# First block's up projection by seven block products, its context work moved, and token tiles taken in pairs

## The chip, the cores and the metric

The kernel runs on one core of a Trainium2 chip, in one launch. The metric is device time in microseconds, the lower the better; three runs of the kernel before took 2593.44, 2595.51 and 2596.91 us, so its median is 2595.51 us.

## The reference, cut to what matters

Two transformer blocks run one after the other over 1024 tokens of width 1024, all in fp32. What the change touches:

```
# first block
mix = token_mixer(x)                          # attention, then y @ w_out
x1  = layer_norm(ALPHA * x + mix)
u   = x1 @ w_up                               # 1024 x 5632: 22 chunks of value, 22 of gate, 128 wide
u   = u[t]*w2 + u[t-1]*w1 + u[t-2]*w0 + b     # causal convolution of width 3 along the tokens
x2  = layer_norm(ALPHA * x1 + (value * gelu(gate)) @ w_down)
# second block
shift, scale, gate ... = modulation of a conditioning vector (6 x 1024 sums)
h   = rmsnorm(x2) * g * (1 + scale) + shift   # then gated linear attention, two directions, whose
                                              # start states come from 256 context tokens
x   = x2 + gate * (gla(h) @ w_o)
x   = x + gate2 * (relu(norm(x) @ w1)**2 @ w2) ; out = rmsnorm(x) * final_g
```

## The kernel before, in words

Every matrix product is done with operands cut in two rounded halves (`split`: one copy on ScalarE gives the high half, one subtraction on VectorE the low half), and `mm3` (lines 131 to 133) issues three matmuls for one product: high by high, high by low and low by high. One 128-row step of a product over 512 columns is so three matmuls.

The program is one stream of stages. (1) Attention, to about 503 us. (2) `mixed`: the product with w_out by token tile (`square_product`, 2 halves of the columns, 8 tiles of 128 tokens, 24 matmuls each), and beside it `context`, the start states from the context tokens; behind each tile's second half comes its layer norm and the transposed halves `hi` and `lo` (lines 828 to 837). (3) `ffn`: for each of 22 chunks the two up products (`up`, line 855: 8 row steps by 2 halves by 3 matmuls, 48 for one 128-wide column chunk), the convolution from PSUM (lines 911 to 913), gelu and product, and in groups of three chunks the down product (`down`, line 864), which adds into the 8 resident tiles `res`. The modulation sums (`ada`) go out in small bits behind each chunk's convolution. The last group runs by tile and feeds the norm and the first values of stage (4), the gated linear attention. (5) `o_projection`: the product with w_o and the operands of the next stage, tiles 0 to 7 in order. (6) `mlp_up`: the second block's up projection, two 128-wide chunks at a time as a 2 by 2 block matrix times the 2 by 2 blocks of the activations, by seven block products of 12 matmuls (84 for a pair of chunks) where plain products would take eight (96). It needs sums and differences of the blocks, made on VectorE (`operands` and lines 1237 to 1242); the partial results go through the two output tiles `ga` and `gb`, which alternate between two sets of `res` tiles. (7) `mlp_down`, groups of four chunks read back from DRAM.

The order of instructions on each engine is laid down by the framework's planner, which takes the program order as priority and simulated times for what is ready. Each engine runs its queue in order; PE waits where a PSUM bank is still to be read. Tile pools are stacked, and a pool that is opened takes over the space of the one closed; with `reuse_waits="tile"` a tile waits only for the tiles that lay in its own bytes. The steps that the change touches: `mixed` 817 to 842, `up` and `down` 855 to 893, `ffn` 895 to 1005, `o_projection` 1127 to 1187, `mlp_up` 1211 to 1266, `mlp_down` 1271 to 1318.

Of the kernel before, what the change touches and what calls it, by code (L numbers as in the profile page):

```python
# [17 lines left out]
P = 128  # L18
D = 1024
# [35 lines left out]
def build(tc, I, out, dbg=None, stop=None):  # L55
# [41 lines left out]
    hi = actp.tile([P, KD, T], F32R, name="act_hi")  # L97
    lo = actp.tile([P, KD, T], F32R, name="act_lo")
# [459 lines left out]
    rawp, wp = pool(w_st, "wraw2", 4), pool(w_st, "wsplit2", 4)  # L558
# [62 lines left out]
    def square_product(wname, wo, done, scale=None, ks=range(KD)):  # L621

        W = I[wname]
        for half in range(2):
            ws = []
            for k in ks:
                r = wo.tile([P, 512], F32, tag="raw", name="woraw", bufs=2)
                SP.dma_start(out=r, in_=W[k, half])
                h = wo.tile([P, 512], F32R, tag="h", name="woh")
                l = wo.tile([P, 512], F32R, tag="l", name="wol")  # L630
                split(r, h, l, None if scale is None else scale[:, k:k + 1])
                ws.append((h, l))
            for t in range(NT):
# [4 lines left out]
                yield 5200  # L638
# [104 lines left out]
    def context(st):  # L743

        nonlocal gc, gt, ge, gv, gs
        gc = pool(st, "cc", 1)
        gt, ge, gv, gs = (pool(st, n, b) for n, b in (("gtc", 2), ("gec", 4), ("gvc", 4), ("gsc", 2)))
# [4 lines left out]
        for t in range(2):  # L752
            x, f = res[6], res[7]
# [63 lines left out]
    def mixed():  # L817
        st = ExitStack()
        set_banks(st, "m", {"c": (1, 2, "z hps fp tokp"), "ct": (1, 1, "ctp ktp dS"), "tp": (1, 2, "xtp"), "sq": (1, 3, "sq")})
        wo = pool(st, "wo", 8)  # L820
        aux = pool(st, "aux", 1)
# [6 lines left out]
        def done(t, half, psum):  # L828
            c = slice(half * 512, half * 512 + 512)
            if half == 0:  # L830
                mv[t] = aux.tile([P, 6], F32, name=f"mv{t}")
                SP.dma_start(out=res[t], in_=I["x"][toks(t), :])
                POOL.tensor_scalar(out=res[t], in0=res[t], scalar1=ALPHA, scalar2=0.0, op0=ALU.mult, op1=ALU.add)
            add_sum(res[t][:, c], psum, res[t][:, c], mv[t][:, half:half + 1])
            if half == 1:
                layer_norm(res[t], mv[t], g, b, junk, POOL if t < 6 else DVE)
                transposed(res[t], t)

        merge([(square_product("w_out", wo, done, ks=(4, 5, 6, 7, 0, 1, 2, 3)), 83200), (context(st), CTXSHARE)])
        st.close()  # L840

    mixed()

    def dump_res(key):
        for t in range(NT):
            SP.dma_start(out=dbg[key][toks(t), :], in_=res[t])
        ctx.close()

    if stop == "x1":
        return dump_res("x1")  # L850
# [4 lines left out]
    def up(w, name):  # L855
        w = w_get(w)
        psum = acc("up", T)
        for half in range(2):
            c = slice(half * 512, half * 512 + 512)
            for k in range(KD):  # L860
                mm3(psum[:, c], *w[k], hi[:, k, c], lo[:, k, c], k == 0, k == KD - 1)
        return psum

    def down(chs, g, wds, wdr, wdp, evac, tile_outer, by_col=None):
        def load(ch, half):
            r = wdr.tile([P, 512], F32, tag="r", name="wdraw")
            SP.dma_start(out=r, in_=wds[2 * ch + half])
            if by_col is not None:
                POOL.tensor_tensor(out=r, in0=r, in1=by_col[:, half * 512:half * 512 + 512], op=ALU.mult)
            h = wdp.tile([P, 512], F32R, tag="h", name="wdh")  # L870
            l = wdp.tile([P, 512], F32R, tag="l", name="wdl")
            split(r, h, l)
            return h, l

        def one(t, half, ws):
            psum = acc("down")
            for n, ch in enumerate(chs):
                gh, gl = g[ch]
                mm3(psum, gh[:, toks(t)], gl[:, toks(t)], *ws[n], n == 0, n == len(chs) - 1)
            evac(t, half, psum)  # L880

        if tile_outer:
            ws = [[load(ch, half) for ch in chs] for half in range(2)]
            for t in range(NT):
                for half in range(2):
                    one(t, half, ws[half])
                yield t
        else:
            for half in range(2):
                ws = [load(ch, half) for ch in chs]  # L890
                for t in range(NT):
                    one(t, half, ws)
                yield half

    def ffn():
        st = ExitStack()
        set_banks(st, "f", {"mm": (1, 2, "down"), "tp": (1, 2, "xtp ada"), "big2": (2, 1, "up tokp"), "big": (2, 1, "up tokp")})
        wdp = pool(st, "wdp", 6)
        ar = pool(st, "ar", 2)
        ac = pool(st, "ac", 1)  # L900
        gp = pool(st, "gp", 4)
        wdr = pool(st, "wdr", 2)
        cp = pool(st, "cp", 2)
        Wu, Wd = wlist("w_up"), wlist("w_down")
        groups = [list(range(i, min(i + 3, NCH))) for i in range(1, NCH, 3)]
        groups = [[0]] + groups

# [506 lines left out]
```

## Time and profile before

| what | us |
|---|---|
| median of 3 runs | 2595.51 |
| the profiled execution | 2593.83 |
| its span, first to last instruction | 2592.1 |
| PE busy in it | 2513.0 |
| VectorE (DVE) busy | 1471.6 |
| ScalarE (ACT) busy | 1053.2 |
| GpSimd (POOL) busy | 437.8 |

A row of the windows view gives a stretch of the span, its length, and for each engine the busy time and the number of instructions; PEclk is the clock that TensorE was granted as a share of full speed. A row of the view by line gives source line, engine, operation, output and inputs by the program's names, shape and count, then the busy time in us and the mean of one in ns, then the idle time of that engine just before these instructions and what ended it. In a timeline the first two numbers are start and duration in us. A matmul's duration overlaps with the next; its cost in a full stream is the distance of starts.

### The profile page before, as it was taken

Reading aid. Unit: us, or ns where it says so; the run is one execution under the profiler, and the core shown is the slowest. Engines: PE = TensorE matmul, PEld = TensorE weight load, DVE = VectorE, ACT = ScalarE, POOL = GpSimd, SP = SyncE. Lnnn points to the kernel's source line nnn. Section 1 sums busy time; section 2 is a strip of 40 time slices with the busy share of each in tenths; the row PEclk is TensorE's granted clock in tenths of the full one; section 3 lists DMA queues with packets and bytes.
Section 4 is the critical chain, followed back from the end, with each engine's and each line's share of the span. In section 5 each row is a group of like instructions: output and inputs, shape, how many; then the busy total and the mean of one; then the engine's idle time right before and its main releaser. Section 6 shows DMA issues by size and latency. Waiting matters only on the chain.

```text
span 2592.1 us, 35515 instructions
## 1 busy us (share of the span) xinstructions
PE 2513.0 (97%) x13114; PEld 2134.0 (82%) x13114; DVE 1471.6 (57%) x2757; ACT 1053.2 (41%) x1956; POOL 437.8 (17%) x583
## 2 busy tenths in 40 slices
PE   8999999899999999999998999999969999899998
PEld 7898988788788888888887888998858888688887
DVE  5767666758564555455557856444374444344466
ACT  5555555745221222222226644333355454421212
POOL 4675622423000000000006100000110000000023
PEclk9999999999999999999999999999989999999999
DMA  5334231532322222222222110112323232532222
GB/s 173 98 96 112 78 82 49 168 114 78 102 88 70 75 79 68 67 83 69 76 73 86 54 37 32 32 44 62 117 90 122 98 106 90 203 103 93 99 100 102
DMA packets 124718, 231.13 MB, mean 89 GB/s; under 512 B 15608, under 2 KB 47992, under 8 KB 124544
## 3 DMA queue, kind: packets, MB, share of 16 engines
q1 hardware_dynamic: 124544, 228.86, 27.5%
q8 instruction: 103, 1.69, 0.3%
q14 instruction: 71, 0.58, 0.1%
HBM read 185.25 MB, written 35.16 MB: 85 GB/s over the span
## 4 chain that ended last, share of the span: by engine, by line
PE 60%; issue 31%; DVE 3%; POOL 2%; DMA 2%; ACT 1%; SPq 0%; POOLq 0%; DVEq 0%; ACTq 0%
PE down L131 5%; PE down L132 5%; PE down L133 5%; PE s L131 4%; PE s L133 4%; PE s L132 4%; PE proj L131 3%; PE proj L133 3%; PE proj L132 3%; PE tokp L132 2%; PE tokp L133 2%; PE tokp L131 2%; PE y L416 2%; PE ptp L91 2%; PE sq L131 1%
## 5 line engine op out<-in xcount | busy, mean ns | idle before, releaser
L131 PE MATMUL down<-wdh,gh 128*128 128x512 f32 x864 | 338.8, 392 | 12.0 <-ACT gh L103 11.0
L132 PE MATMUL down<-wdl,gh 128*128 128x512 f32 x864 | 338.0, 391 | 0.3 <-DVE wdl L104 0.2
L133 PE MATMUL down<-wdh,gl 128*128 128x512 f32 x864 | 334.1, 390 | 0.2 <-DVE gl L104 0.2
L103 ACT CAST wh<-raw 128x512 fp32r<-128x512 f32 (+2 forms) x204 | 125.9, 622 | 416.1 <-PE up L132 366.7
L131 PE MATMUL up<-act_hi,wh 128*128 128x512 f32 x704 | 279.1, 397 | 3.3 <-DVE conv L913 2.5
L132 PE MATMUL up<-act_lo,wh 128*128 128x512 f32 x704 | 278.4, 395 | 0.0
L133 PE MATMUL up<-act_hi,wl 128*128 128x512 f32 x704 | 277.5, 394 | 0.0
L570 POOL TENSOR_TENSOR rstd<-rstd,mhalf 128x1 f32<-128x1 f32 x74 | 50.2, 678 | 1247.1 <-DVE rstd L569 1230.4
L104 DVE TENSOR_TENSOR wl<-raw,wh 128x512 fp32r<-128x512 f32 (+2 forms) x204 | 155.3, 769 | 158.9 <-ACT wh L103 152.3
L131 PEld LDWEIGHTS down<-wdh,gh 128*128 128x128 f32 x864 | 162.8, 188 | 48.6 <-ACT gh L103 11.5
L132 PEld LDWEIGHTS down<-wdl,gh 128*128 128x128 f32 x864 | 162.9, 189 | 35.2 <-DVE wdl L104 1.3
L133 PEld LDWEIGHTS down<-wdh,gl 128*128 128x128 f32 x864 | 162.2, 188 | 34.7 <-DVE gl L104 0.6
L131 PEld LDWEIGHTS up<-act_hi,wh 128*128 128x128 f32 x704 | 133.2, 189 | 33.0 <-ACT conv L911 2.9
L133 PEld LDWEIGHTS up<-act_hi,wl 128*128 128x128 f32 x704 | 133.1, 189 | 30.1
L132 PEld LDWEIGHTS up<-act_lo,wh 128*128 128x128 f32 x704 | 133.1, 189 | 29.6 <-DVE act_lo L615 0.4
L131 PE MATMUL tokp<-wh,act_hi 128*128 128x256 f32 (+1 forms) x512 | 148.0, 290 | 0.0
L132 PE MATMUL tokp<-wl,act_hi 128*128 128x256 f32 (+1 forms) x512 | 147.6, 289 | 0.0
L133 PE MATMUL tokp<-wh,act_lo 128*128 128x256 f32 (+1 forms) x512 | 146.5, 287 | 0.0
L1289 DVE TENSOR_TENSOR res<-res,down 128x512 f32<-128x512 f32 x112 | 76.7, 685 | 115.7 <-PE down L133 115.5
L103 ACT CAST wdh<-wdraw 128x512 fp32r<-128x512 f32 x108 | 65.6, 621 | 166.6 <-PE down L133 75.0
L922 DVE TENSOR_TENSOR res<-res,down 128x512 f32<-128x512 f32 x96 | 65.4, 686 | 111.8 <-PE down L133 111.6
L370 ACT ACTIVATE P<-P,mx 128x640 f32<-128x640 f32 (+7 forms) x128 | 94.4, 738 | 78.9 <-DVE mx L367 74.1
(325 smaller groups left out, 6209.4 us busy)
## 6 DMA issues: line engine op xcount, KB each, us to landing
ada_w<-in_ada_w SPq DMA_DIRECT2D x192, 128.0 KB, 2.1
raw<-in_w_up SPq DMA_DIRECT2D x88, 256.0 KB, 2.6
res<-in_mlp_w SPq DMA_DIRECT2D x32, 512.0 KB, 3.6
gd<-res SPq DMA_DIRECT2D x32, 512.0 KB, 4.2
wdraw<-in_mlp_w SPq DMA_DIRECT2D x64, 256.0 KB, 3.7
gload<-gd SPq DMA_DIRECT2D x32, 512.0 KB, 4.3
wdraw<-in_w_down SPq DMA_DIRECT2D x44, 256.0 KB, 2.7
raw<-in_wqk SPq DMA_DIRECT2D x32, 256.0 KB, 3.0
```

What stands on the lines that cost most here:

```text
L91: PE.transpose(out=o, in_=a, identity=ident)
L103: ACT.copy(h, raw)
L104: DVE.tensor_tensor(out=l, in0=raw, in1=h, op=ALU.subtract)
L131: PE.matmul(out=o, lhsT=ah, rhs=bh, start=first, stop=False, **kw)
L132: PE.matmul(out=o, lhsT=ah, rhs=bl, start=False, stop=False, **kw)
L133: PE.matmul(out=o, lhsT=al, rhs=bh, start=False, stop=last, **kw)
L370: ACT.activation(Pm[:, 0:W], Pm[:, 0:W], AF.Exp, bias=mx[:, 0:1], scale=-1.0, accum_out=mx[:, 1:2])
L416: PE.matmul(out=o, lhsT=lhsT, rhs=part[:, off:off + w], start=(first and n == 0 and m == 0), stop=(last and n == len(cur) - 1 and m == 1))
L570: POOL.tensor_tensor(out=t[:, 1:2], in0=t[:, 0:1], in1=mhalf, op=ALU.pow)
L922: DVE.tensor_tensor(out=r, in0=r, in1=psum, op=ALU.add)
L1289: DVE.tensor_tensor(out=r, in0=r, in1=psum, op=ALU.add)
```

## The change

The first block's up projection becomes the same seven-product routine as the second block's (`up_pass`, shared by both), as a pass of its own over 22 pairs (value chunk, gate chunk). Its results are written to DRAM (`g1d`), and the down product becomes a pass behind it (`down_group`, shared too) that reads them back, with groups of 2, 2 and six of 3 chunks. The context states and the modulation leave the w_out stage and the up pass and run beside the first seven groups of that down pass; the activations `hi` and `lo` are given up after the up pass and allocated anew. The layer norm's output goes to DRAM (`x1d`) and is added in the last group but one. In the two stages that make the operands, token tiles run as 0, 4, 1, 5, 2, 6, 3, 7, so that each pair's operands can be made as soon as both tiles are there; part of their work goes from VectorE and ScalarE to GpSimd. The first weight chunk of each up pass is loaded and split ahead into a pool of its own (`w0`). In the second block the gate vector multiplies the columns of w_o instead of the result. The pools of both down passes stand in another order.

```diff
+    PAIRED = (0, 4, 1, 5, 2, 6, 3, 7)
+    def square_product(wname, wo, done, scale=None, by_col=None, ks=range(KD)):
...
+                if by_col is not None:
+                    POOL.tensor_tensor(out=r, in0=r, in1=by_col[:, half * 512:half * 512 + 512], op=ALU.mult)
...
+            for t in PAIRED:
+    def operands(t, E, sp):
+        if t < 4:
+            return split(by_k(res[t]), hi[:, :, toks(t)], lo[:, :, toks(t)])
+        t -= 4
+        b1, b2 = res[t], res[t + 4]
...
+        POOL.tensor_tensor(out=s[:, XS], in0=b2[:, XS], in1=b1[:, XS], op=ALU.subtract)
+        DVE.tensor_tensor(out=b2[:, XS], in0=b2[:, YS], in1=b2[:, XS], op=ALU.subtract)
+        split(by_k(b2), hi[:, :, toks(t + 4)], lo[:, :, toks(t + 4)])
+        DVE.tensor_tensor(out=s[:, YS], in0=b2[:, YS], in1=s[:, XS], op=ALU.subtract)
+        split(by_k(s), E[0][:, 0:8, toks(t)], E[1][:, 0:8, toks(t)])
+        POOL.tensor_tensor(out=u, in0=b1[:, YS], in1=s[:, YS], op=ALU.subtract)
+        split(by_k(u), E[0][:, 8:12, toks(t)], E[1][:, 8:12, toks(t)])
+    def up_pass(W, pairs, E, w0, room, finish):
+        first = load(0)
+        A1 = parts(first[0], w0)
+        yield
...
+            X, Z, Y = acc("s"), acc("s"), acc("s")
+            product(X, A11, "B11", True)
+            ACT.copy(ga[:, XS], X)
+            product(Z, A12, "B21", True)
+            DVE.tensor_tensor(out=ga[:, XS], in0=Z, in1=ga[:, XS], op=ALU.add)
+            product(X, S2, "T2", False)
+            ACT.copy(ga[:, YS], X)
+            product(Y, S1, "T1", True)
+            product(X, S3, "T3", False)
+            ACT.copy(gb[:, YS], X)
+            DVE.tensor_tensor(out=gb[:, YS], in0=Y, in1=gb[:, YS], op=ALU.add)
+            product(Y, S4, "B22", False)
+            DVE.tensor_tensor(out=ga[:, YS], in0=Y, in1=ga[:, YS], op=ALU.add)
+            product(X, A22, "T4", False)
+            ACT.copy(gb[:, XS], X)
+            finish(n, ga, gb)
...
+                DVE.scalar_tensor_tensor(out=r, in0=r, scalar=m[:, 2:3], in1=g, op0=ALU.add, op1=ALU.mult)
+                SP.dma_start(out=x1d[t], in_=r)
+                rows(r, t)
+                operands(t, E, sp)
+        up = up_pass(wlist("w_up"), NCH, E, w0, lambda n: (res[n % 2], res[4 + n % 2], res[2], res[6]), conv_gate)
...
+    def conv_gate(n, gv_, gg_):
+        o = res[3], res[7]
+        for i, (psum, x) in enumerate(zip((gv_, gg_), o)):
+            c = convc[:, 2 * n + i, :]
+            ACT.activation(x, psum, AF.Identity, scale=c[:, 2:3], bias=c[:, 3:4])
+            DVE.scalar_tensor_tensor(out=x[:, 1:T], in0=psum[:, 0:T - 1], scalar=c[:, 1:2], in1=x[:, 1:T], op0=ALU.mult, op1=ALU.add)
+            DVE.scalar_tensor_tensor(out=x[:, 2:T], in0=psum[:, 0:T - 2], scalar=c[:, 0:1], in1=x[:, 2:T], op0=ALU.mult, op1=ALU.add)
+        gelu = ACT.activation(o[1], o[1], AF.Gelu_apprx_tanh)
+        DVE.tensor_tensor(out=o[0], in0=o[0], in1=o[1], op=ALU.mult)
+        SP.dma_start(out=g1d[n], in_=o[0])
...
+        wdr, gr, gp, wdp = pools = [pool(st, n, b, reuse_waits="tile") for n, b in (("wdr", 2), ("gr", 2), ("gp", 4), ("wdp", 6))]
+        groups = [[0, 1], [2, 3]] + [list(range(i, i + 3)) for i in range(4, NCH, 3)]
...
+                    if n == last - 1:
+                        x = wdr.tile([P, 512], F32, tag="r", name="x1res")
+                        SP.dma_start(out=x, in_=x1d[t][:, c])
+                        DVE.scalar_tensor_tensor(out=r, in0=x, scalar=ALPHA, in1=r, op0=ALU.mult, op1=ALU.add)
...
+            POOL.tensor_scalar(out=res[t], in0=res[t], scalar1=rs, scalar2=0.0, op0=ALU.mult, op1=ALU.add)
+            rows(res[t], t, vec["gs1"], vec["sh1"])
+            split(by_k(res[t]), hi[:, :, toks(t)], lo[:, :, toks(t)])
...
+        merge([(most(), 207024), (context(cst), CTXSHARE), (modulation(), 144)])
...
-        gr, gp, wdr, wdp, rp, fc = (pool(st, n, b, reuse_waits="tile") for n, b in (("gr", 2), ("gp2", 8), ("wdr2", 4), ("wdp2", 8), ("rp2", 2), ("fc2", 1)))
+        wdp, wdr, gr, gp, rp, fc = (pool(st, n, b, reuse_waits="tile") for n, b in (("wdp2", 6), ("wdr2", 2), ("gr2", 2), ("gp2", 8), ("rp2", 2), ("fc2", 1)))
```

## Rows read from the trace of the kernel before

**Rows 1.** The page, busy time of each engine, share of the span, instructions.
```profile
PE 2513.0 (97%) x13114; PEld 2134.0 (82%) x13114; DVE 1471.6 (57%) x2757; ACT 1053.2 (41%) x1956; POOL 437.8 (17%) x583
```
**Rows 2.** Windows by stage: stretch, length, busy time (instructions) per engine, PEclk, DMA share, GB/s.
```profile
503.50:652.00 148.50, 143.65 (x797) 123.49 (x795) 99.60 (x211) 71.66 (x156) 44.29 (x34) 0.98 0.37 123
652.00:720.00 68.00, 63.08 (x255) 50.49 (x256) 34.84 (x48) 20.93 (x30) 1.75 (x2) 0.92 0.26 83
720.00:1360.00 640.00, 640.00 (x2811) 525.30 (x2810) 348.31 (x476) 157.91 (x194) 0.00 (x0) 1.00 0.24 75
1360.00:1440.00 80.00, 72.56 (x404) 61.53 (x404) 54.50 (x105) 49.10 (x111) 51.35 (x50) 0.98 0.21 77
1911.00:2223.70 312.70, 310.85 (x1344) 253.85 (x1344) 142.65 (x177) 151.03 (x190) 0.00 (x0) 0.99 0.30 100
2223.70:2592.10 368.40, 350.41 (x1537) 289.52 (x1536) 188.19 (x257) 91.49 (x147) 40.92 (x32) 0.98 0.35 119
```
**Rows 3.** By line, PE: up products of the first and of the second block.
```profile
L131 PE MATMUL up<-act_hi,wh 128*128 128x512 f32 x704 | 279.1, 397 | 3.3 <-DVE conv L913 2.5 <-DVE mv L587 0.4 <-ACT act_hi L612 0.3
L131 PE MATMUL s<-act_hi,uh 128*128 128x512 f32 x256 | 100.6, 397 | 11.4 <-ACT uh L103 11.4
L131 PE MATMUL s<-ext_hi,uh 128*128 128x512 f32 x192 | 75.9, 395 | 1.8 <-ACT uh L103 1.1 <-ACT res L1255 0.7
```
**Rows 4.** Timeline of DVE in the second block's up pass, two pairs apart.
```profile
2010.24 0.69 DVE L1256 TENSOR_TENSOR res<-s,res 128x512 f32<-128x512 f32 x1 [5.19 <-ACT res L1255]
...
2048.69 0.69 DVE L1256 TENSOR_TENSOR res<-s,res 128x512 f32<-128x512 f32 x1 [5.19 <-ACT res L1255]
```
**Rows 5.** Window of these two pairs.
```profile
2010.24:2048.69 38.45, 38.45 (x170) 31.55 (x169) 17.92 (x22) 19.16 (x24) 0.00 (x0) 1.00 0.33 110
```
**Rows 6.** By line: the first block's convolution and gate product.
```profile
L912 DVE SCALAR_TENSOR_TENSOR conv<-up,convc,conv 128x1023 f32<-128x1023 f32 x44 | 56.4, 1282 | 14.8 <-ACT conv L911 14.8
L911 ACT ACTIVATE conv<-up,convc 128x1024 f32<-128x1024 f32 x44 | 53.0, 1203 | 0.6 <-PE up L133 0.6
L976 DVE TENSOR_TENSOR conv<-conv 128x1024 f32<-128x1024 f32 x22 | 26.9, 1224 | 6.6 <-ACT conv L973 6.6
```
**Rows 7.** By line: a three-operand DVE pass with both tensors in SBUF.
```profile
L107 DVE SCALAR_TENSOR_TENSOR wol<-woraw,ghead,woh 128x512 fp32r<-128x512 f32 x16 | 12.0, 750 | 12.9 <-ACT woh L106 12.9
```
**Rows 8.** Windows: from w_o's last matmul to the second up pass, and its start.
```profile
1886.70:1911.00 24.30, 4.08 (x25) 3.20 (x23) 21.70 (x27) 18.96 (x38) 4.22 (x4) 0.65 0.31 95
1911.00:1918.00 7.00, 5.82 (x13) 4.10 (x14) 6.93 (x10) 3.57 (x5) 0.00 (x0) 0.51 0.30 110
```
**Rows 9.** Windows: from the second up pass to the second down pass.
```profile
2223.70:2234.90 11.20, 0.17 (x1) 0.00 (x0) 3.37 (x6) 5.45 (x8) 0.00 (x0) 0.71 0.97 325
2234.90:2239.00 4.10, 4.08 (x10) 3.26 (x11) 4.03 (x5) 2.60 (x4) 0.00 (x0) 0.53 1.05 414
```
**Rows 10.** Timeline of the DMA queue there: first chunks read back.
```profile
2225.23 1.69 SPq L1314 DMA_DIRECT2D gload<-gd  x2
```
**Rows 11.** The page's DMA issues: size and us to landing.
```profile
gd<-res SPq DMA_DIRECT2D x32, 512.0 KB, 4.2
```
**Rows 12.** By line, DVE from 503 to 655 us: what is not context.
```profile
L587 DVE CUSTOM_DVE_ANT_0 res<-sq,res 128x512 f32<-128x512 f32 x16 | 10.9, 683 | 14.3 <-PE sq L133 14.3
L582 DVE TENSOR_TENSOR res<-res,ln1g 128x1024 f32<-128x1024 f32 x7 | 10.7, 1535 | 2.1 <-POOL res L581 2.1
L615 DVE TENSOR_TENSOR act_lo<-xtp,act_hi 128x512 fp32r<-128x512 f32 x14 | 9.1, 682 | 0.5 <-ACT act_hi L612 0.5
```
**Rows 13.** By line, DVE: modulation, down sums, split of down weights.
```profile
L162 DVE SCALAR_TENSOR_TENSOR ada_acc<-ada_w,cs,ada_acc 128x256 f32<-128x256 f32 x112 | 54.0, 483 | 20.3 <-DMA ada_w<-in_ada_w 18.3
L922 DVE TENSOR_TENSOR res<-res,down 128x512 f32<-128x512 f32 x96 | 65.4, 686 | 111.8 <-PE down L133 111.6
L104 DVE TENSOR_TENSOR wdl<-wdraw,wdh 128x512 fp32r<-128x512 f32 x108 | 75.5, 718 | 28.7 <-ACT wdh L103 28.5
```
**Rows 14.** By line, POOL: a weight chunk times a row of column factors.
```profile
L869 POOL TENSOR_TENSOR wdraw<-wdraw,m5b 128x512 f32<-128x512 f32 x8 | 13.0, 1641 | 608.8 <-DMA wdraw<-in_mlp_w 608.8
```

More of the change, by code (lines that the diff above doesn't have):

```diff
@@ L557, in build @@
     small = pool(ctx, "small", 4)
-    rawp, wp = pool(w_st, "wraw2", 4), pool(w_st, "wsplit2", 4)
+    x1d = [tc.dram_tile([P, D], F32, name=f"x1d{t}") for t in range(NT)]
     x2d = [tc.dram_tile([P, D], F32, name=f"x2d{t}") for t in range(NT)]
@@ L835, in done @@
+            add_sum(r[:, c], psum, r[:, c], mv[t][:, half:half + 1])
             if half == 1:
-                layer_norm(res[t], mv[t], g, b, junk, POOL if t < 6 else DVE)
-                transposed(res[t], t)
-        merge([(square_product("w_out", wo, done, ks=(4, 5, 6, 7, 0, 1, 2, 3)), 83200), (context(st), CTXSHARE)])
-        st.close()
[L842 to L906, printed above, removed]
-        def conv(psum, i, tag):
-            o = cp.tile([P, T], F32, tag=tag, name="conv")
-            c = convc[:, i, :]
-            ACT.activation(o, psum, AF.Identity, scale=c[:, 2:3], bias=c[:, 3:4])
-            DVE.scalar_tensor_tensor(out=o[:, 1:T], in0=psum[:, 0:T - 1], scalar=c[:, 1:2], in1=o[:, 1:T], op0=ALU.mult, op1=ALU.add)
-            seen.append(DVE.scalar_tensor_tensor(out=o[:, 2:T], in0=psum[:, 0:T - 2], scalar=c[:, 0:1], in1=o[:, 2:T], op0=ALU.mult, op1=ALU.add))
-            return o
+                m = mv[t]
@@ L916, in evac @@
         def evac(n):
             def f(t, half, psum):
[L918 removed]
+                c = slice(half * 512, half * 512 + 512)
+                r = res[t][:, c]
                 if n == 0:
[L920 to L921 removed]
+                    return ACT.copy(r, psum)
+                if n < last:
                     DVE.tensor_tensor(out=r, in0=r, in1=psum, op=ALU.add)
[L923 to L928 removed]
@@ L946, in norm1 @@
+                    return
+                if half == 0:
+                    mv[t] = sums()
+                add_sum(r, psum, r, mv[t][:, half:half + 1])
+                if half == 1:
+                    layer_norm(res[t], mv[t], *gb, junk[0])
+                    SP.dma_start(out=x2d[t], in_=res[t])
+            return f
         def norm1(t):
-            xn = cp.tile([P, D], F32, tag="cg", name="xn")
             rs = rms_of(res[t], junk[0])
-            POOL.tensor_scalar(out=xn, in0=res[t], scalar1=rs, scalar2=0.0, op0=ALU.mult, op1=ALU.add)
@@ L1267, in build @@
-    mlp_up()
+                xn = sp.tile([P, D], F32, tag="s", name="xn2")
+                rs = rms_of(r, xn)
+                POOL.tensor_scalar(out=xn, in0=r, scalar1=rs, scalar2=0.0, op0=ALU.mult, op1=ALU.add)
+                rows(xn, t, vec["gs2"], vec["sh2"])
+                operands(t, E, sp)
+        up = up_pass(wlist("mlp_w1"), NMLP // 2, E, w0, lambda n: tuple(res[i + n % 2] for i in (0, 4, 2, 6)), relu2)
+        for t, half in square_product("w_o", wo, done, scale=ghead, by_col=m):
+            if half == 1 and t == 5:
+                next(up)
@@ L1268, in build, with relu2 @@
+        st.close()
+        return up
+    g2d = [tc.dram_tile([P, T], F32, name=f"g2d{c}") for c in range(NMLP)]
+    def relu2(n, ga, gb):
+        for i, g in enumerate((ga, gb)):
+            ACT.activation(g, g, AF.Relu)
+            ACT.activation(g, g, AF.Square)
+            SP.dma_start(out=g2d[2 * n + i], in_=g)
+    w0 = pool(w0_st, "w02", 1)
+    E = open_ext(ext_st, "ext2")
+    drain(o_projection(E, w0))
+    w0_st.close()
     ext_st.close()
@@ L1281, in mlp_down @@
         bcast(fg, "final_g")
+        ss = {}
         def evac(n):
@@ L1307, in evac @@
             return f
[L1309 removed]
         for n, chs in enumerate(groups):
[L1311 to L1317 removed]
+            drain(down_group(chs, g2d, W2, pools, evac(n), n == last, m5 if n == last else None))
         st.close()
```

356 lines of the change are left out of this document (163 added, 193 removed).

## The prediction

> **What bounds the kernel now.** I read the page's busy times first: PE is busy 97% of the span, the next engine 57% [rows 1]. Then windows by stage, to see where PE is not full [rows 2]. From 720 to 1360 us, the first block's up and down products, it never stops at full clock. It falls short only where stages meet. The total of matmuls decides, and after it the price of each turn.
>
> What one matmul costs: in the second block's up pass the same add recurs after 38.45 us, two pairs of chunks later [rows 4], and PE is busy all that time [rows 5]. A pair is 84 matmuls, so 38.45 / 168 = 0.2289 us each.
>
> **The change, part by part.** The sum is made against the profiled execution, 2593.8 us (span 2592.1 and 1.7 around it); the median shown is 1.7 above it.
>
> *Matmuls.* The first block's up products are 3 x 704 = 2112; the second's are 3 x (256 + 192) = 1344 for 16 pairs, 84 a pair [rows 3]. By the new routine the first block has 22 x 84 = 1848. 264 fewer x 0.2289 = **-60.4**. Context, modulation, transposes and down products keep their PE work.
>
> *The w_out stage loses the context.* 148.5 us with PE busy 143.65 [rows 2]; most of the 4.9 us idle belongs to context chains that wait in it: **-4** (0 to -5).
>
> *First turn, norm to up pass.* Before, 652 to 720 us: 4.9 us idle, and 63 us at clock 0.92, another 5; so 10 us lost [rows 2]. After, the first two products need the high halves of tiles 0 to 3, the third the sums from tile 7. Behind tile 3's last matmul stand the norm, the store of x1d, and, because `rows` writes over the tile that is being stored, a wait for that store (4.2 us for 512 KB [rows 11]); its transposes hide under it. I put the first product 6 us behind the stage's last matmul (an estimate: some 11.6 us of chain from tile 3, less the 5.6 us of tile 7's matmuls). The clock has fallen to 0.51 behind such a gap [rows 8], so the 24 matmuls cost 24 x 0.2289 / 0.51 = 10.8 us where 5.5 are due. 6 + 5.3 - 1 (transposes done meanwhile) + 2 for the queues, since DVE has about 11.7 us of work in the 12.6 us of a tile pair: 12 lost, **+2**. Bounds: -5 (tile 3 ready at once) to +17 (as dear as the second block's turn today, 27).
>
> *Up pass.* DVE is busy 17.92 us and ACT 19.16 in two pairs [rows 5]: 9.0 and 9.6 a pair, of which relu and square on ACT go. Added a pair: four convolution passes of 1.28 and one product of 1.22 on DVE, 6.35; on ACT three passes, 3.4 [rows 6]. DVE comes to 15.3 of 19.2 us, 80%: full, but under PE. The passes now read `ga`, `gb` from SBUF instead of PSUM. For a pass with both tensors in SBUF the row is 0.75 us for 512 columns [rows 7], so 0.53 more for 1023: 1.28, unchanged.
>
> The Trainium skill says otherwise ("Vector Engine (DVE) Microarchitecture Reference", section "Points that are easy to get wrong"): such a pass with two non-bf16 SBUF sources runs at half rate. Four passes would then take twice 1.28, DVE would need 20.4 us of a 19.2 us pair, and the sum would be 1.2 x 22 = 26 us higher. The row at 0.75 us speaks against it: half rate would be about 1.3.
>
> The new wait: `ga` and `gb` are one set, where the second block has two. The next pair's first copy from PSUM into `ga` waits until the convolution has read it, and behind that copy stands PE's third product. Chain from the pair's sixth product: add 0.69, ACT 1.2, two DVE passes 2.56, copy 0.6, about 5 us. PE has for that time the seventh product and three of the next pair that need no `ga` (first, second, fourth): 12 matmuls or 2.75 us each, 11 us. Splits of the next weights in the DVE queue (2.4 us and more) take part of that cover. I take 0.23 us a pair, **+5** (0 to 5 x 22 = 110 if nothing is issued ahead).
>
> *New turn, up pass to down pass.* The second block has one: 11.0 us idle and 4.1 us at clock 0.53, 13 lost [rows 9]. There the chunks are asked for only at 2225.2 us, after the last matmul [rows 10], in space that the last weights held. In the new order the raw tiles lie where the sums of weights lay, which are done with a pair earlier; chunk and weight are loaded in turn, and a first group has two chunks. One split of 1.05 us and little more stays: **+3** (1 to 13).
>
> *The down pass with context and modulation.* PE: 19 chunks x 48 x 0.2289 = 209 us, and about 50 us of context and modulation products, 259. DVE: the w_out stage's 99.6 us [rows 2] less adds 10.9, norm 10.7, low halves 9.1 [rows 12] and 12 weight splits of 0.7 leaves 60 for context; modulation 54.0 and 8 more; six groups of down sums 65.9; the new x1 pass 16 x 0.69 = 11; chunk splits 19 x 1.22 = 23; weight splits 38 x 0.7 = 27 [rows 6, 13]. Together 249, 96% of PE's time. DVE also waited 18.3 us for modulation weights [rows 13], and it may now wait for the x1 loads, which share two buffers with the down weights. Each tile's PSUM bank is freed by a DVE add, and there are three. All these loads stand in the one queue of SP: some 240 at 0.85 us each at most [rows 10], 204 of 259 us. 249 + 18 is 8 us over PE, and queues this full cost some more: **+14** (0 to 30).
>
> *Last group and norm.* 1360 to 1440 us lost 7.4 us [rows 2]. POOL copies become ACT and DVE work; the norm now writes over the tile that is being stored to x2d and waits for it (4.2 [rows 11]). **0** (-5 to +5).
>
> *Second block.* POOL now multiplies each w_o chunk, 1.64 us [rows 14], before its split: the first comes about 3 us later, beside transposes; the rest stay under four tiles' matmuls a chunk (2.75 us). **+3** (0 to 6). The turn there costs 24.3 us with 4.08 busy and then 7 at clock 0.51 [rows 8], 27 by the whole stage (from 1886.7 to 2223.7 us, less 1344 x 0.2289, less 2 of transposes). DVE is busy 21.7 of these 24.3 us and ACT 19.0: it is a backlog. Each of tiles 4 to 7 puts about 5.9 us of operand work on DVE (three or four subtractions of 0.69, three splits), all begun behind the fourth tile. In pairs, it starts at the second tile, over 45 us of matmuls, and POOL and DVE take part of the rest. Then a chain of about 4 us and 24 matmuls at half clock are left, 10 lost: **-17** (-22 to -6).
>
> *Second down pass.* The new pool order as above: 13 lost becomes 4, **-9** (-11 to 0).
>
> Sum: -60.4 - 4 + 2 + 5 + 3 + 14 + 0 + 3 - 17 - 9 = -63.4; 2593.8 - 63.4 = 2530.4, and with the 1.7 to the median **2532 us**.
>
> **The rivals.**
> 1. *Slower: the single set of `ga`, `gb` breaks the overlap.* Today two pairs overlap, since each has its own output tiles; the planner's order might put the convolution behind the splits, so that PE stands through the chain of 5 us in each pair: +105, 2637 us. It decides from 63.4 / 22 + 0.23 = 3.1 us a pair. For it: DVE at 80%, in order. Against: 11 us of matmuls that need no `ga`.
> 2. *DVE becomes the bound of the first block.* 1 us lost in each pair (17 more) and 34 instead of 14 in the down pass: 2569 us. For it: the 96%. Against: modulation has no reader before the second block, so it can be put off.
> 3. *The turns stay dear.* The first block's turn like the second's today (+15), the new turn at 13 (+10), no gain at the second block's two (+26): 2583 us. For it: every turn so far was lost at low clock. Against: DVE busy 89% in the one, a late load in the other; both causes are changed.
> 4. *Everything fits.* No DVE loss, no pair loss, new turn and w_o at nothing: 2532 - 5 - 14 - 3 - 3 = 2507 us.
> 5. *Passes on two SBUF tensors at half rate*: 2558 us.
>
> **How the numbers follow.** Forecast 0.58; rival 1 0.06, rival 2 0.17, rival 3 0.08, rival 4 0.09, rival 5 0.02. The range 2505 to 2577 us holds the forecast, rivals 2, 4 and 5. Left out: rivals 1 and 3, and tails of the others, 0.18. No change is within 0.2% (2590.3 to 2600.7 us), about what a measurement of this kernel can tell from none. Slower: rival 1 beyond its point, and a sum of rivals 2 and 3: 0.06. Same: the edge between, 0.04. Faster: 0.90.
>
> **What would show it.** The up pass's matmuls 1848, and the same add every 38.4 us over two pairs: right; 40 or more with PE waiting for ACT's copy: rival 1 or 2. DVE above 93% from the first down matmul to the last group, with PE waits on DVE sums of 5 to 15 us. The first convolution pass at 1.28 us. Idle before each up pass 4 to 8 us instead of 20 in the second block, and both down passes starting within 4 us of the last up matmul. A sum of waits in the up pass above 60 us would make the forecast wrong; so would a turn of more than 20 us.

## The result and the profile after

The changed kernel takes 2687.71 us (median of 4 runs, 2683.45 to 2695.06), the kernel before 2596.21 in the same session: ratio 1.0357, 95% interval 1.0332 to 1.0382. The forecast was 2532 us; the sign was wrong. The profiled execution takes 2686.0 us (span 2684.3).

The page's busy times, beside [rows 1]: PE did 24 us less and stood 196 us of the span instead of 79.

```profile
PE 2488.7 (93%) x12850; PEld 2094.4 (78%) x12850; DVE 1606.8 (60%) x2951; ACT 1146.1 (43%) x2026; POOL 464.9 (17%) x591
```

Windows by stage of the changed kernel, columns as in [rows 2]: start of the w_out stage; the rest of it; first turn; up pass; new turn; down pass with context and modulation; its end; norm and first products of the next stage; second turn; last part of the second down pass.

```profile
503.60:521.00 17.40, 7.24 (x19) 5.72 (x20) 3.05 (x6) 3.21 (x6) 8.36 (x8) 0.61 0.78 301
521.00:611.00 90.00, 89.78 (x406) 72.17 (x404) 39.91 (x67) 29.87 (x43) 24.90 (x14) 1.00 0.22 76
611.00:672.00 61.00, 35.79 (x141) 28.16 (x141) 46.57 (x57) 26.05 (x36) 14.00 (x9) 0.75 0.22 78
672.00:1105.00 433.00, 392.05 (x1663) 308.88 (x1662) 290.44 (x311) 187.86 (x220) 0.00 (x0) 1.00 0.19 70
1105.00:1145.00 40.00, 26.02 (x88) 19.36 (x87) 23.81 (x29) 19.88 (x27) 0.72 (x1) 0.79 0.46 157
1145.00:1365.00 220.00, 214.48 (x1104) 181.20 (x1103) 168.61 (x358) 85.46 (x170) 3.23 (x5) 1.00 0.56 181
1365.00:1430.00 65.00, 51.59 (x207) 40.16 (x205) 44.12 (x78) 6.47 (x8) 0.00 (x0) 0.90 0.60 183
1430.00:1560.00 130.00, 115.47 (x588) 97.32 (x587) 104.62 (x235) 77.72 (x151) 39.62 (x35) 0.93 0.18 65
1950.00:2020.00 70.00, 38.70 (x165) 30.86 (x164) 53.80 (x75) 35.66 (x60) 25.14 (x18) 0.73 0.32 107
2600.00:2684.00 84.00, 65.14 (x277) 52.54 (x275) 46.52 (x74) 15.01 (x40) 32.32 (x26) 0.92 0.29 103
```

Before, PE never stopped from 720 to 1360 us; now it loses 41 us in the up pass at full clock. DVE is nowhere as full as forecast: 67% in the up pass (80% was forecast), 77% in the main part of the down pass (96%). What PE waited for in the whole run (us, times, longest):

```profile
PE xtp L91 <- POOL xn L1253: 30.6, 4, 13.3
PE s L130 <- ACT res L744: 27.7, 21, 1.4
PE xtp L91 <- DVE res L1005: 17.3, 2, 8.7
PE s L130 <- ACT res L747: 15.5, 22, 1.3
...
PE down L130 <- ACT wdh L102: 12.1, 4, 4.9
PE sq L130 <- ACT woh L102: 10.2, 1, 10.2
PE down L130 <- ACT gh L102: 8.0, 2, 6.9
...
PE tokp L132 <- DVE act_lo L103: 6.4, 6, 2.2
```

For all that follows, one table of stretches in us. Each is worked out from the first or last recorded product of a stage on PE; a turn is the time from the last product of the square stage to the 166th up product, less 168 x 0.2289 (some records are missing, so it is good to about 2 us). e8 and h1 are kernels of the next section.

| stretch | before | after | e8 | h1 |
|---|---|---|---|---|
| attention's end to first w_out product | 0.0 | 10.2 | 5.4 | 5.2 |
| first turn | 16.2 | 34.5 | 32.3 | 26.3 |
| first up pass, first to last product | | 492.2 | 428.5 | 432.1 |
| gap to the down pass | | 6.9 | 8.3 | 9.2 |
| first down pass | | 333.1 | 321.6 | 313.5 |
| from there to the first w_o product | 377.4 | 394.6 | 388.8 | 395.9 |
| second turn | 27.6 | 40.8 | 43.9 | 27.5 |
| gap to the second down pass | 11.0 | 1.0 | 3.2 | 10.3 |
| second down pass to the end | 357.2 | 370.1 | 373.2 | 358.2 |

### The profile page after: what moved, and what is told of

Its sections match the earlier page's. It is cut to its first block, busy times and chain, and to the rows that moved or that the text cites. A ratio compares the mean times of both kernels' runs of the same rounds, so it can differ in the third digit from the quotient of the medians.

```text
span 2684.3 us, 35315 instructions
## 1 busy us (share of the span) xinstructions
PE 2488.7 (93%) x12850; PEld 2094.4 (78%) x12850; DVE 1606.8 (60%) x2951; ACT 1146.1 (43%) x2026; POOL 464.9 (17%) x591
## 4 chain that ended last, share of the span: by engine, by line
PE 76%; DVE 8%; DMA 5%; issue 4%; ACT 4%; POOL 3%; SPq 0%; DVEq 0%; POOLq 0%; ACTq 0%
PE s L130 9%; PE s L131 9%; PE s L132 9%; PE down L130 6%; PE down L131 6%; PE down L132 6%; PE proj L130 3%; PE proj L132 3%; PE proj L131 3%; PE y L415 2%; PE tokp L132 2%; PE tokp L130 2%; PE tokp L131 2%; PE ptp L91 2%; PE S L361 1%
## 5 line engine op out<-in xcount | busy, mean ns | idle before, releaser
L130 PE MATMUL s<-act_hi,uh 128*128 128x512 f32 x608 | 240.8, 397 | 28.1 <-ACT res L744 27.7
L131 PE MATMUL s<-act_lo,uh 128*128 128x512 f32 x608 | 239.2, 393 | 0.4 <-DVE act_lo L103 0.4
L132 PE MATMUL s<-act_hi,ul 128*128 128x512 f32 x608 | 234.2, 394 | 0.0
L130 PE MATMUL s<-ext_hi,uh 128*128 128x512 f32 x456 | 182.0, 400 | 23.5 <-ACT res L747 15.5
L103 DVE TENSOR_TENSOR ul<-res,uh 128x1024 fp32r<-128x1024 f32 x76 | 94.8, 1248 | 142.8 <-ACT uh L102 142.8
L132 PE MATMUL s<-ext_hi,ul 128*128 128x512 f32 x456 | 179.5, 396 | 0.7 <-DVE ul L103 0.7
L131 PE MATMUL s<-ext_lo,uh 128*128 128x512 f32 x456 | 180.0, 395 | 0.0
L130 PEld LDWEIGHTS s<-act_hi,uh 128*128 128x128 f32 x608 | 115.2, 189 | 61.8 <-ACT res L744 36.7
L131 PEld LDWEIGHTS s<-act_lo,uh 128*128 128x128 f32 x608 | 115.0, 189 | 25.9 <-DVE act_lo L103 0.9
L132 PEld LDWEIGHTS s<-act_hi,ul 128*128 128x128 f32 x608 | 114.9, 189 | 24.9
```

Of the source, the lines that this page charges most:

```text
L103: DVE.tensor_tensor(out=l, in0=raw, in1=h, op=ALU.subtract)
L130: PE.matmul(out=o, lhsT=ah, rhs=bh, start=first, stop=False, **kw)
L131: PE.matmul(out=o, lhsT=ah, rhs=bl, start=False, stop=False, **kw)
L132: PE.matmul(out=o, lhsT=al, rhs=bh, start=False, stop=last, **kw)
```

## The experiments

Each later group starts from the best of the one before. The kernel before had medians of 2596 to 2598 us beside them; a ratio is to these. Each edit is shown shortened to its core.

**One set of `ga`, `gb`.**

```
+ if finish is conv_gate and n % 2:
+     if n == 1: spare = [w0.tile([P, D], F32, tag=x) for x in ("wh", "wl")]
+     ga, gb = spare
```

> Odd pairs of the first block's up pass get a second set of ga and gb (in the tiles that held the first weights); nothing else is changed. Theory A (one set): PE waits 27.7 + 15.5 us in this pass for ACT's copies into ga and gb, because a copy may not start before the convolution of the pair before has read the tile. With two sets these waits fall below 8 us, a pair takes 19.3 to 19.8 us instead of 21.75, and the total falls by 38 to 50 us, to 2638 to 2650. Rival B (DVE and ACT, 14.4 us and about 9 us of work a pair in queues kept in order, are late whatever the tile): the waits on the copies only move to the adds, a pair stays above 21 us, and the total stays within 10 us of 2688.

2628.26 us (ratio to before 1.0124, 1.0102 to 1.0146): 59 us gained, theory A and more. In the pass PE is now full, and both waits are gone:

```profile
660.00:1040.00 380.00, 380.00 (x1662) 311.79 (x1661) 282.95 (x312) 183.85 (x220) 0.00 (x0) 1.00 0.22 78
```

Why so small a wait cost so much is in one pair of the changed kernel. ACT, then PE, the two stops of a pair:

```profile
811.47 0.59 ACT L740 COPY res<-s 128x512 f32<-128x512 f32 x1 [1.45 <-DVE res L1032]
813.19 1.05 ACT L102 CAST uh<-res 128x1024 fp32r<-128x1024 f32 x1 [1.14 <-PE s L131]
815.94 1.04 ACT L102 CAST uh<-s 128x1024 fp32r<-128x1024 f32 x1 [1.70 <-PE s L131]
816.89 0.58 ACT L744 COPY res<-s 128x512 f32<-128x512 f32 x1
820.59 0.59 ACT L747 COPY res<-s 128x512 f32<-128x512 f32 x1 [3.12 <-PE s L132]
```
```profile
817.52 0.50 PE L130 MATMUL s<-act_hi,uh 128*128 128x512 f32 x1 [1.39 <-ACT res L744]
821.23 0.51 PE L130 MATMUL s<-ext_hi,uh 128*128 128x512 f32 x1 [0.68 <-ACT res L747]
```

The first copy (L740) stands until the convolution (L1032) has left `ga`. That chain is 6.9 us long, from the last sum into `ga` at 805.18 to the copy's end at 812.06, where 5 were forecast, since DVE works the passes of `gb` first:

```profile
805.18 0.69 DVE L750 TENSOR_TENSOR res<-s,res 128x512 f32<-128x512 f32 x1 [0.67 <-PE s L132]
```

PE does not stand for this copy: it has products for that time. But it uses them up. So the pairs are worked one behind the other, and at the two later copies no product of another pair lies between a copy and the product that goes on in its bank: PE stands for the bare copy, once with a cast of 1.04 us ahead of it. 1.39 + 0.68 in nearly each of 22 pairs are the 43.2 us of the list. From start to start a stop costs a little more than its idle time: the product at 817.52 has its like one pair on at 839.38, 21.86 us later, where a pair in e1 takes 19.23, which is 84 x 0.2289. So 2.63 us are lost in a pair. Besides, the last pair waits 5.7 us for its first copy (PE behind L740). From the 166th up product to the last, the time above 1682 x 0.2289 is 62.2 us after the change and 1.3 in e1: 61 in these two traces, 59 in the medians.

**The start of the w_out stage, a buffer, an order.**

```
e2: - wo, aux, sp = pool(wo), pool(aux), pool(sp)   + aux, sp, wo = ...
e3: - xn = sp.tile(tag="s")  (2 buffers)            + xn = sp.tile(tag="xn")  (1 and 1)
e4: + for i in tail: hold.enter_context(tc.issue_after(i.ins))   # n in (1, 2)
```

> Order of three pools in the w_out stage: the weights last instead of first, so that they lie 16 KB higher; nothing else is changed. Theory A (space): the weights are asked for only at 505.5 us (492.3 before the change), since their tiles lie where attention still works. Higher up they are asked for before 496 us, the first product follows attention's last within 1 us instead of 10.2, and the total falls by 9 to 14 us, to 2674 to 2679. Rival B (queue): they stand behind the loads of x in SP's queue, which go at 503.6 us; then the first product stays at 513 to 514 us and the total within 3 us of 2688.

2691.77 us: neither. The weights' first load goes at 503.4 instead of 505.5 us, the first product is still 9.9 us late. Whether the higher place was free is not shown: the loads of the norm's vectors (L618) now have the low place, wait there for attention until 501.5 us, and stand ahead of the weights in SP's queue.

```profile
SPq L618 <- DVE pl L402: 25.7, 1, 25.7
```

This edit moved something else, unlooked for: the first turn is 27.3 us instead of 34.5. The planner put the sums of the first up weights behind the last norms on DVE, while the split beside POOL's add is as dear as after the change. First the kernel after the change, then e2:

```profile
619.69 0.68 DVE L731 TENSOR_TENSOR s<-res 128x512 f32<-128x512 f32 x1
636.17 1.27 DVE L1005 SCALAR_TENSOR_TENSOR res<-res,rstd,ln1b 128x1024 f32<-128x1024 f32 x1
```
```profile
612.35 3.24 DVE L103 TENSOR_TENSOR act_lo<-res,act_hi 128x1024 fp32r<-128x1024 f32 x1
625.75 1.28 DVE L1005 SCALAR_TENSOR_TENSOR res<-res,rstd,ln1b 128x1024 f32<-128x1024 f32 x1
638.60 1.29 DVE L731 TENSOR_TENSOR s<-res 128x512 f32<-128x512 f32 x2
```

The last norm (L1005) ends 17.7 us behind the last w_out product, after the change 26.3. The total gains nothing by it, since the first down pass takes 343.3 us instead of 333.1 and the second turn is 3.6 longer; why is not shown.

> In the second block's turn the normalised tile gets a buffer of its own (one for it, one for the sums) instead of two shared ones; nothing else is changed. Theory A (shared buffers): tile 7's square, due at 1983.5 us, starts at 1992.5, when the sums of the tile before are split; apart, PE's waits for the normalised tile fall from 30.6 us to 18 to 22 and the total by 8 to 13 us, to 2675 to 2680. Rival B (order on DVE): the same chains wait for DVE, where 0.15 us of statistics stand behind 8 us of work on the up weights; then the waits stay above 27 us, and the total within 4 us of 2688, or above it, since one buffer each lets fewer tiles overlap.

2697.2 us, 10 slower: theory A in this form is wrong. The second turn is 47.7 us; that one buffer each lets fewer tiles overlap is the likely reason.

> In both blocks the ACT and DVE work on the up weights of the second and third pair is put behind the last split of the eighth tile's sums; nothing else is changed. Theory A (DVE backlog in the turns): between 612 and 640 us DVE does about 9 us of such work, and as much between 1957 and 1992, ahead of the norms of the last tiles; held back, each turn is 7 to 12 us shorter, the total 14 to 24 us, 2664 to 2674. Rival B (the turns are a chain of waits for stores and buffers, DVE's work beside it): each turn is less than 3 us shorter and the held work comes late, so that PE waits at the second pair; the total is 2682 to 2700.

2685.5 us: rival B. The turns are 33.7 and 37.4 us; PE waits 7.3 us for the held weights instead. Only the second and third pair were held: the sums of the first pair stay ahead of the last norms (at 616.9 to 624.1 us), which e2 had behind them.

**What the first turn does not depend on** (on e1; turns there 34.7 and 45.1).

```
e5: SP.dma_start(out=x1d[t], in_=r) moved to the load of x
e6: - for t in PAIRED:   + for t in range(NT):      # both square products
e7: POOL.tensor_tensor(subtract) -> DVE.tensor_tensor   # in operands
```

> e1, with x1d stored at the start of the w_out stage, when the tile holds x, instead of behind the norm: as much traffic, but nothing in the first turn waits for a store (x1d holds x instead of x1, so the residual of the first block is left wrong). Theory A (rows writes over the tile that is being stored): ACT's copies of the sixth and the eighth tile wait 4.9 and 8.5 us in the queue, 4.3 and 4.9 of it for the store; without them the stretch from the last w_out product (619 us) to the first sums product (649 us) is 7 to 10 us shorter, and the total falls from 2628 to 2617 to 2622. Rival B (DVE's and POOL's queues are as late themselves): less than 4 us are gained, 2624 to 2632.

2635.95 us: rival B, and worse: 3 us less in the turn (31.7), but the stage ahead takes 5.8 us longer, with these stores among its loads.

> e1, with the token tiles in the order 0 to 7 in both square products instead of in pairs (this undoes that part of the change). Theory A (pairs make the turns dear: tile 3, which the first two products need, ends beside tile 7 instead of four tiles earlier, and two tiles' norms share DVE's queue at the very end): both turns get shorter, the second to the 24 to 27 us that it cost before the change, the total falls by 10 to 25 us to 2603 to 2618. Rival B (pairs do help, as my forecast had it: the operands of four tiles would all be worked behind the stage's last products): each turn is 5 to 15 us longer, 2638 to 2658.

2631.88 us: neither. The turns are 38.1 and 42.7 us. The order of the tiles, which I had thought the cure of the turns, is worth nothing either way as the kernel stood then, with the other chains still in it.

> e1, with the two subtractions of each tile pair that the change gave to POOL back on DVE (as before the change). Theory A (POOL's 1.3 to 2.7 us each, slowed by DVE and slowing it, lie in the chain of the last tile, and DVE takes 0.68): each turn is 2 to 5 us shorter, the total 4 to 10 us, 2618 to 2624. Rival B (DVE is the full engine of the turns, 36.3 of 39 us in the first): 1.4 us more on it for each of four tiles costs each turn 2 to 5 us, 2632 to 2638.

2627.74 us, no difference; the turns are 32.3 and 45.8 us.

**Loads.**

```
e8: + with tc.issue_after(fourth[0].ins): SP.dma_start(out=r, in_=I["x"]...)
    - x = wdr.tile(tag="r", name="x1res")   + x = xr.tile(tag="x", name="x1res")   # 4 buffers
```

> e1 with two edits in stages far apart, each read in its own stage. (1) The loads of x in the w_out stage are issued behind the fourth load of w_out weights: theory A (the weights' first two loads, issued at 505.5 us, arrive only at 513 since 4 MB of x stand ahead of them on the DMA engines): the first product comes at 507 to 509 us instead of 513.8, 5 to 7 us; rival: the place is not free earlier, the first product moves by less than 2 us. (2) The halves of x1 in the down pass come into four buffers of their own instead of the two of the down weights: theory A: PE's waits for down weights in this pass (about 5 us at one place, and more behind it) go, 4 to 8 us; rival (SP's queue, with some 240 loads in line, is late itself): less than 2 us. Both together by theory A: 2613 to 2619; by the rivals 2625 to 2631.

2607.93 us (1.0044, 1.003 to 1.0058), 20 gained: (1) near theory A, (2) beyond it. Below, SP's queue before the change, where weights went ahead of x; after it, where two weight loads stand among 4 MB of x, half of it ahead of them; and PE in e8. The first product comes 7 us earlier than at 513.76, but attention ends 2.4 us earlier here too: the gap behind it is 5.4 us instead of 10.2 (9.1 in e1).

```profile
492.33 0.81 SPq L628 DMA_DIRECT2D woraw<-in_w_out  x2
```
```profile
503.64 1.75 SPq L995 DMA_DIRECT2D res<-in_x  x4
505.50 1.24 SPq L629 DMA_DIRECT2D woraw<-in_w_out  x2
506.79 2.94 SPq L995 DMA_DIRECT2D res<-in_x  x4
```
```profile
506.55 2.08 PE L130 MATMUL sq<-woh,act_hi 128*128 128x512 f32 x4 [5.40 <-ACT woh L102]
```

The waits for down weights in the first down pass, 15.5 us in e1, are gone from e8's list, where those for split chunks lead: loads of x1 had stood in the weights' two buffers. First e1, then e8:

```profile
PE down L130 <- ACT wdh L102: 15.5, 4, 6.8
```
```profile
PE down L130 <- ACT gh L102: 11.1, 2, 8.3
```

The pass is 13 us shorter than in e1, the step from it to w_o 6.

**The second turn and the second down pass.**

```
e9:  + SP.dma_start(out=r, in_=x2d[t])  # whole, behind the eighth weight; x2res goes
     - ("wdp2", 6), ("wdr2", 2)   + ("wdp2", 8), ("wdr2", 4)
e10: - if t in (3, 7):   + if True:    # norm's last step on DVE; and e7's edit
e11: + drain(most(0, 1)) ahead of merge([(most(1, last), ...
e12: e4's edit
```

> e8 with two more edits, stages apart. (1) w_o stage: x2 is loaded whole into the token tile's own place behind the eighth weight, as the first block does with x, instead of in halves through one buffer. Theory A: the last w_o product ends at 1962.3 us after the change, but its sum is added only at 1971.8, since each half waits for the load that the add before it set free; with x2 there ahead the add follows within 1.5 us, and the turn (from the last w_o product until the first two pairs are done, less 168 x 0.2289) falls from 43.9 us in e8 to 32 to 36. Rival: DVE's and POOL's queues are late by as much, the turn stays above 40 us. (2) Second down pass: eight pairs of split weights and four raw ones, as before the change, instead of six and two. Theory A: from its first product to the end it takes 357 us as before the change, instead of 370 to 373. Rival: less than 3 us. Together by theory A 2584 to 2592; by the rivals 2604 to 2610.

2596.55 us, level with before (0.9997, 0.9982 to 1.0012). The turn fell by 6.3 us, to 37.6: half of theory A. The changed kernel's rows show that half; DVE adds the last sums, SP loads each half only when the one before is added (the last product ended at 1962.3):

```profile
1965.03 0.68 DVE L1248 TENSOR_TENSOR res<-sq,x2res 128x512 f32<-128x512 f32 x1
1971.81 0.68 DVE L1248 TENSOR_TENSOR res<-sq,x2res 128x512 f32<-128x512 f32 x1
```
```profile
1966.10 0.43 SPq L1247 DMA_DIRECT2D x2res<-x2d  x1
```

The down pass is back at 357.2 us from 373.2, but the gap ahead of it at 10.0 from 3.2.

> e9 with the last step of the norm in the w_out stage on DVE for every token tile (it was so for the last pair; the other six went over ACT and POOL), and the subtractions of the tile pairs on DVE in both turns. Theory A (POOL and DVE slow each other: the same split of 1024 columns takes 1.21 us alone and 1.7 to 3.2 beside a POOL operation, POOL's add 3.3): DVE's rows go back to 1.2 to 1.3 us, and the first turn falls from 32 to 34 us to 24 to 28; the total is 5 to 10 us below e9. Rival (DVE is simply full): 7.6 us more DVE work makes the turn longer, 0 to 6 us above e9.

2595.6 us. Theory A for the first turn (27.1 us), and undone in the second (44.3 us), where the subtractions are better on POOL.

> e9 with the first group of the down pass written out ahead of the context and the modulation, so that its loads stand before most of theirs in SP's queue. Theory A (the first chunk is asked for at 1131.5 us, behind ten loads of the context that wait for space): the wait of 6.9 to 8.3 us for the first split chunk falls below 4, the total is 3 to 8 us below e9. Rival (space: the chunk's place comes free only with the last sums of weights, or the context then comes late and leaves gaps behind): within 3 us of e9 or above it.

2593.44 us (0.9981, 0.997 to 0.9991). 3 less, but not for the reason of theory A: PE still waits up to 8.3 us for the first split chunk; the pass behind it is 9 us shorter.

> e9 with the up weights of the second and third pair held back as in e4. Theory A (with loads and buffers out of the way, DVE's queue is what ends last in the turns): each turn 3 to 8 us shorter, the total 6 to 14 us below e9. Rival (as in e4: what is held back is then waited for): within 3 us of e9.

2596.16 us: rival, as in e4.

**Why the turns stayed dear.**

```
h1: e11 + first block's part of e10;  POOL.tensor_scalar(out=r, in0=r ...), rms_of(r, junk)
h2: as h1, but xn = sp.tile(tag="xn")  # one buffer, square into junk
h3: h1, pools wdh2, fc2, wdr2, gr2, wdl2, gp2, rp2 in this order
```

> e11, with the first block's norm and subtractions on DVE as in e10 (second block's subtractions stay on POOL), and in the second turn the norm in the tile's own place with the square written into a small tile of its own, as before the change. Theory A (the shared buffers make the tiles a chain: eight squares at 1851.8 to 1910.8 us, the last four 8 to 13 us apart, though their sums were there 20 us earlier): the last square follows the last sum within 5 us and the second turn falls from 37.8 us to 25 to 30. First turn 26 to 29 instead of 33.7 (as in e10). Total 2574 to 2582. Rival (POOL held up by DVE sets the pace: its power of one column took 6.7 us beside DVE where it takes 0.55 alone): the second turn stays above 34 us, total 2584 to 2590.

2579.13 us (0.9928, 0.9913 to 0.9942). Theory A: second turn 27.5, first 26.3. ACT's last squares in the changed kernel (the last sum at 1971.81) and in h1 (its last product ends at 1872.0):

```profile
1982.35 1.05 ACT L590 ACTIVATE xn<-res 128x1024 f32<-128x1024 f32 x1
1992.50 1.06 ACT L590 ACTIVATE xn<-res 128x1024 f32<-128x1024 f32 x1 [2.81 <-DVE ext_lo L103]
```
```profile
1871.90 1.06 ACT L590 ACTIVATE junk<-res 128x1024 bf16<-128x1024 f32 x1
1880.03 1.06 ACT L590 ACTIVATE junk<-res 128x1024 bf16<-128x1024 f32 x1 [5.58 <-issue]
```

After the change the last square came 20.7 us behind the last sum and 30.2 behind the last product, since it writes into the buffer of the normalised tile, which is shared with the sums: square, norm, transposes and splits of one tile had to be over before the next tile's square. In h1 it comes 8 us behind the last product. The turn is then as dear as before the change (27.6), not cheaper; in h1 PE waits most of it for POOL's norm, which was not taken apart:

```profile
PE xtp L91 <- POOL res L1265: 18.4, 2, 17.4
```

> As h1, but the normalised tile keeps one buffer of its own, and only the square goes elsewhere; so nothing waits for the store of h ahead of the norm, and the tiles' norms follow each other through one buffer. Theory A (the square in that buffer made the chain): second turn 26 to 31 us, total 2574 to 2583. Rival (the buffer itself, from norm to transposes, makes it): 34 us or more, total 2584 to 2590.

2580.96 us, second turn 32.1: nearer theory A, a little over its range. It is the square more than the buffer of the norm: PE's waits for the normalised tile fall from 27.6 us in e11 to 8.2. But 4.6 us of h1's gain are missing, PE waits 10.5 us for split up weights (4.8 in h1), and whether the one buffer has a part in that is not shown.

> h1, with the pools of the second down pass in another order: high halves of the weights first, then the raw weights and chunks where the up pass keeps the sums of weights, the low halves behind. Theory A (place and number of buffers are a trade: six and two came free early, but are too few; eight and four are enough, but the raw ones lie where the last weights are): the gap from the last up product to the first down product falls from 10 to 12 us to 2 to 5, the pass itself stays at 357 us, the total is 6 to 9 us below h1. Rival (with more loads the queue is what is late): the gap stays above 8 us, within 3 us of h1.

2576.17 us (0.9914, 0.9897 to 0.993), the fastest. PE's waits around the second down pass, after the change, in e9 and in h3:

```profile
PE down L130 <- ACT wdh L102: 4.9, 1, 4.9
PE down L131 <- DVE wdl L103: 1.8, 2, 1.1
PE down L130 <- ACT gh L102: 1.0, 1, 1.0
```
```profile
PE down L130 <- ACT wdh L102: 10.0, 1, 10.0
```
```profile
PE down L130 <- ACT gh L102: 3.9, 1, 3.9
```

The gap is 3.9 and the pass 357.0 us: place and number were one trade, theory A. Of the 6 to 9 us only 3 are in the medians, whose intervals overlap.

## Why the prediction was wrong

The sum was forecast as -63 and is +92 us against the trace of before. Right was the largest term, the matmuls: 1848 up products are recorded in the first block, and e1 has them at 0.2286 each. The convolution reads two SBUF tensors at 1.28 us a pass, unchanged from [rows 6] (the row gives count, then shortest, median and longest in ns):

```profile
L1031 DVE SCALAR_TENSOR_TENSOR res<-res,convc,res x44: 1274/1276/1286, 674.9 to 1137.4; 128x1023 f32<-128x1023 f32 x44
```

Rival 5, and with it the Trainium skill's half rate for such a pass ("Vector Engine (DVE) Microarchitecture Reference", section "Points that are easy to get wrong"), does not hold in this trace. Nearly every other term of the sum was too low:

- *Up pass, +5.* This step failed most: it measured 62 (59 by e1's medians). I compared the chain of 5 us with 11 us of matmuls that need no `ga`, as if these stood ready beside it. They had to come first in PE's order; behind the late first copy nothing of another pair was left to cover the next two. It was rival 1, which I gave 0.06, by its heading and not by its mechanism: PE stood for the late copy once, and else for the two copies behind it, 2.63 us a pair instead of 5.
- *Turns, +2 and -17.* They came out at +18 and +13. The first: my 11.7 us of DVE work in 12.6 counted each operation at its time alone. In the changed kernel a split of 1024 columns took 3.24 us beside POOL's add; in h1, with only one-column operations left on POOL there, all are at 1.21 to 1.22. POOL is not all of it: e2's turn is as short (27.3) with POOL's add in place, and there the first up weights were worked behind the norms. The prediction names no such work in this turn. The second: I freed the backlog on DVE, but the square and the norm in a ring of two, and x2 in a single buffer, put the tiles in a chain that no engine's busy time shows. Without both (h1) the turn costs what it did before, so the 17 us were not had even then; what still holds it is open. Tile order, on which I rested them, was worth nothing (e6). Rival 3 had these two turns, though not the gaps ahead of the down passes, for a weaker reason.
- *w_out stage, -4.* The 4.9 us of idle time did go (0.2 left from 521 to 611 us), but 10.2 came at the stage's start: about +5. Before, the first weights were asked for at 492.33 and the first product stood right behind attention; now they came late and among the loads of x, which I did not price. e8 took 5 of it back; there the weights wait for their place until 503.0.
- *Down pass, +14.* I named the x1 loads in the buffers of the down weights, and then put the price on DVE at 96%. It was the buffers: 13 us of e8's gain lie in the pass and 6 in the step behind it. DVE was 77% busy.
- *Last group and norm, 0.* From the last down product to the first of w_o it takes 17 us longer. 12 of them have passed when the last first-value product ends (46.0 us behind the last down product, 33.9 before). In the kernel before 27 of the 192 first-value products run ahead of that point, now 2; and PE waits 6.4 us in six places for DVE's low halves of the normed tiles, a wait that the kernel before does not show. No experiment was made on it, and the rest stays open.
- *Second down pass, -9.* The gap did fall, from 11.0 to 1.0. But the pass took 12.9 more: six and two buffers are too few for the last group's eight pairs of weights. I read the order of the pools in the diff and passed over their sizes.

From forecast to measurement, in us: up pass 57, turns 16 and 30, start and idle time of the w_out stage 9, gap to the first down pass 4, last group and norm 17, second down pass 12, and the w_o stage -6 (96.3 from its first to its last product, 99.5 before, where +3 was forecast). That makes 139 of the 155. The 16 left over fall to the first down pass; they are a remainder, near the 13 that e8 took from it. Even the fastest kernel here, h3, is 44 us above the forecast: its first turn is some 10 us dearer than before, the second no cheaper, and the step to w_o 21 us longer.

## What to carry to other kernels

A wait is covered only by work that the engine's order has left for that moment: ask what stands between a copy and the next use of its bank, not how much independent work exists. When a stage is rewritten, list every buffer that two uses share and every load that moved ahead of another in the queue, since such chains cost 6 to 60 us each here and no engine's busy share showed them. Changed buffer counts in a diff are a change of their own.

## What the runs showed of the hardware

DVE and POOL held each other up far more than I allowed for. In the changed kernel's first turn, DVE and POOL at the same time (a split of 1024 columns, 1.21 us alone; an add):

```profile
614.17 3.24 DVE L103 TENSOR_TENSOR act_lo<-res,act_hi 128x1024 fp32r<-128x1024 f32 x1
```
```profile
613.01 3.33 POOL L1008 TENSOR_TENSOR res<-res,ln1b 128x1024 f32<-128x1024 f32 x1
```

And in e9 a POOL operation on one column, 0.55 us in the median of 74, lasted through DVE's unbroken row of work:

```profile
1882.31 6.74 POOL L569 TENSOR_TENSOR rstd<-rstd,mhalf 128x1 f32<-128x1 f32 x1 [1.00 <-DVE rstd L568]
```

The Trainium skill ("SBUF — State Buffer", section "SBUF: two separate sides") says that a VectorE operation with two SBUF inputs and a GpSimd one that reads SBUF contend for a shared pair of ports, which the one that starts first holds for its whole instruction while the other stands still. The first two rows agree: the add ends at 616.34, and the split, begun at 614.17, ends 1.07 us behind it, at 617.41. The third row goes further: POOL's operation lasts from 1882.31 to 1889.05, and from 1882.14 to 1888.64 DVE runs eight two-input operations one behind the other; it did not get in between two of them. The mean of 1.64 us for POOL's multiplication [rows 14], 1.29 in the median after the change, fits the same reading.
